# The second feed-forward's way up by seven half products, in two sweeps over pairs of token quarters

## The chip, the core and the metric

The kernel runs on one core of one Trainium2 chip. A core has TensorE for matrix products (PE in the profile, PEld for its weight loads), VectorE (DVE), ScalarE (ACT) and GpSimd (POOL) for elementwise work, and SyncE (SP), which issues the transfers here. Matrix products are summed in PSUM banks; all else lies in SBUF, or in DRAM. The metric is the device time of one execution in microseconds.

## The reference

One step of a transformer trunk layer on 1152 tokens (1024 latent, 128 context) of width 1024. What matters here is its end:

```python
def swiglu(h, w1, w3, w2):
    return (jax.nn.silu(h @ w1) * (h @ w3)) @ w2
...
    x = x + 0.5 * m[2] * swiglu(modulate(x, norm_g[0], m[0], m[1]), *ffn1)
    mix, ctx = token_mixer(modulate(x, norm_g[1], m[3], m[4]), cache, lb, *mixer_w)
    x = x + m[5] * mix
    x = x + 0.5 * m[8] * swiglu(modulate(x, norm_g[2], m[6], m[7]), *ffn2)
```

`w1` and `w3` are 1024 x 2816, `w2` is 2816 x 1024. `modulate` is an RMS norm with a gain and a shift that differ between latent and context tokens. The mixer ends in a merge: two gated up projections are added and go through `w_out`.

## The kernel before

Tokens lie along the free axis, features on the partitions: `x` is eight tiles of 128 x 1152. A product in fp32 accuracy is made of three matmuls in the fast rounded format (`float32r`): each operand is split into a rounded high part and the rest, and high x high, high x low and low x high are summed in one bank (`mm3`, L402; the three matmuls are L406, L407 and L408). A weight is loaded raw by `load_w` (L226), and `hl` (L215) makes its two parts: a cast on ScalarE (L222) and a subtraction on GpSimd (L223). The raw tile has two buffers, the parts (`wh`, `wl`) three each.

The whole runs in stages: first feed-forward, mixer (recurrence, then attention), merge, second feed-forward. The tile framework sorts each engine's queue when the program is built and sets the semaphores.

- `merge` (L1346) makes the up projections and gates tile by tile, three chunks of 384 tokens each, and adds `w_out`'s product to `x` in groups of two feature tiles (`down_group`), the last group chunk by chunk (`down_last`), after which `norm` (L341) makes the next stage's input `xh`, `xl`.
- `ffn` (L631) walks the 22 feature tiles of 128. For each, `up_plain` (L475) makes the gate's product in three chunks, its SiLU (L485), then the other product, their multiplication (L492), and splits the result into `hh`, `hl` (L493 on ScalarE, L494 on GpSimd). They stay in SBUF.
- After every two feature tiles `down_group` (L539) multiplies two older ones with their `w2` rows, 48 products, and adds them to `x` (`down`, L524, the addition on VectorE is L530). So up and down alternate, two feature tiles of each at a time.
- The last four feature tiles go through `down_final` (L571), which holds the final norm and stores the output.

Per feature tile the way up takes 2 x 3 x 24 matmuls of 384 columns, the way down 72.

Of the kernel before, what the change touches and what calls it, by code (L numbers as in the profile page):

```python
# [19 lines left out]
P = 128  # L20
# [16 lines left out]
LB_MIN = 1e-8  # L37

# [31 lines left out]
class Trunk:  # L70
# [3 lines left out]
    def run(self):  # L74
        self.part = {}
        nc, tc, a = self.nc, self.tc, self.a
        with ExitStack() as st:
# [16 lines left out]
            self.mixer()  # L94
            with ExitStack() as s1:
                self.ffn_pools(s1)
                self.ffn(1, 8, 3)
# [64 lines left out]
    def consts(self):  # L162
# [7 lines left out]
        self.mask = cp.tile([P, 5, P], U8, name="mask")  # L170
        mf = self.tt(F32, "maskf")[:, : 5 * P]
        nc.scalar.dma_start(mf, a["mask"])
        nc.vector.tensor_copy(self.mask.rearrange("p a b -> p (a b)"), mf)
        self.ones = cp.tile([P, P], F32, name="ones")
        nc.vector.memset(self.ones, 1.0 / D)
        self.onesb = cp.tile([P, P], F32, name="onesb")
        nc.vector.memset(self.onesb, 0.0)
        nc.vector.memset(self.onesb[0:64, 0:64], 1.0 / 64)
        nc.vector.memset(self.onesb[64:128, 64:128], 1.0 / 64)
        self.onesq = cp.tile([P, P], F32, name="onesq")  # L180
        nc.vector.memset(self.onesq, 1.0 / 384)
        self.onesk = cp.tile([P, P], F32, name="onesk")
        nc.vector.memset(self.onesk, 1.0 / 256)
# [31 lines left out]
    def hl(self, raw, shape, eng=None, pin=lambda i: i, pool=None):  # L215
        if pool:
            w = pool.tile([P, 2, *shape[1:]], F32R, tag="cb", bufs=1, name="wx")
            wh, wl = w[:, 0], w[:, 1]
        else:
            wh = self.wp.tile(shape, F32R, tag="wh", bufs=3, name="wh")  # L220
            wl = self.wp.tile(shape, F32R, tag="wl", bufs=3, name="wl")
# [94 lines left out]
    def rstd(self, r, ps, w=CW):  # L316
        nc = self.nc
        t = self.fp.tile([P, max(w, CW)], F32, tag="hf" if w <= CW else "sq", bufs=2 if w <= CW else 3, name="rt")[:, :w]
# [113 lines left out]
    def ffn_up(self, l, f):  # L432
# [4 lines left out]
        if self.plain:  # L437
            self.up_plain(l, f, hh, hl)
            return hh, hl
# [35 lines left out]
    def up_plain(self, l, f, hh, hl):  # L475
        nc = self.nc
        wa, wb = [partial(self.load_w, self.a["w13"][l, f, j], KT, P) for j in range(2)]

        def gate(c):
            if f or c != ORDER[0]:  # L480
                ps = self.dense(wa, c, "up", 3)
            else:
                ps = drain(self.dense_g(wa, c, "up", 3), self.tail)
            s = self.fp.tile([P, CW], F32, tag="sl", bufs=3, name="sl")
            nc.scalar.activation(s, ps, AF.Silu)  # L485
            return s

        def put(c, s):
            ps = self.dense(wb, c, "up", 3)
            cs = slice(c * CW, (c + 1) * CW)  # L490
            hf = self.fp.tile([P, CW], F32, tag="hf", bufs=2, name="hf")
            nc.vector.tensor_mul(hf, ps, s)  # L492
            nc.scalar.copy(hh[:, cs], hf)  # L493
            nc.gpsimd.tensor_sub(hl[:, cs], hf, hh[:, cs])  # L494
            self.tick()

        wa = wa()
        if f == 0:
            wb = wb()
            for c in ORDER:  # L500
                if c == ORDER[-1]:
                    for _ in self.tail:
                        pass
                s = gate(c)
                for _ in range(3):
                    next(self.tail, None)
                put(c, s)
                for _ in range(2):
                    next(self.tail, None)
        else:  # L510
            sl = [(c, gate(c)) for c in ORDER]
            wb = wb()
            for c, t in sl:
                put(c, t)

# [23 lines left out]
    def down_group(self, w2, fs, hs, gm):  # L539
        ws = [self.load_w(w2[f], 1, D) for f in fs]  # L540
# [966 lines left out]
```

## Time and profile before

| | us |
|---|---|
| median of three runs | 3118.07 |
| lowest and highest | 3117.59, 3119.81 |
| the profiled execution's own time | 3118.19 |
| its span in the trace | 3116.4 |
| merge begins in the trace (first matmul of `ups`) | 2038.5 |
| last matmul of the merge | 2251.0 |
| first matmul of the second feed-forward's way up | 2255.9 |
| last matmul of the way up | 3045.4 |

A group's row gives the line, the engine, the operation, output and inputs by the program's names, the shape and the count, then busy time in us and mean ns of one, then the idle time of the engine before them and what ended it. A row of the timeline gives start and duration in us. A matmul's duration in the trace includes its way through the array, some 0.17 us beyond its share of the array; the distance from one start to the next is what it costs in a stream. Rows with PEld are the weight loads that run beside it. The granted clock is 1.00 at full speed. Rows of the stages give a window, its length, then busy time and count of each engine, the clock, the share of the DMA engines and GB/s.

### The profile page before, as it was taken

How to read it: one execution, taken by the hardware profiler on the slowest of the kernel's cores; microseconds unless marked ns; L12 is line 12 of the kernel's file. 1: busy time of each engine (PE TensorE's matmuls, PEld its weight loads, DVE VectorE, ACT ScalarE, POOL GpSimd, SP SyncE). 2: the span in 40 equal slices, each digit the busy share in tenths (PEclk: the TensorE clock that was granted, in tenths of full speed). 3: DMA queues.
4: the chain of work that ended last, by engine and by line, in shares of the span. 5: the costliest groups of instructions: out<-in, count | busy, mean ns of one | idle time of the engine just before them, and what ended most of it. 6: DMA issues, size and time to landing. Idle time of an engine off the chain costs nothing.

```text
span 3116.4 us, 43157 instructions
## 1 busy us (share of the span) xinstructions
PE 2988.8 (96%) x16896; PEld 2840.4 (91%) x16896; DVE 1743.1 (56%) x3416; ACT 1093.8 (35%) x2029; POOL 1080.0 (35%) x864
## 2 busy tenths in 40 slices
PE   7999999999989999999998999999899999999998
PEld 5999999999988988898997777689899999999997
DVE  7867776675368777777546677744512222222224
ACT  4211111111165554545344777721531111111113
POOL 4322222222243333333235445554542222222224
PEclk9999999999999999999999999999999999999999
DMA  6322222221121111111110001242011111111111
GB/s 239 120 76 82 82 82 81 79 82 54 48 89 45 42 46 42 47 41 47 62 56 12 15 15 32 62 164 84 31 55 41 41 41 44 46 41 41 41 48 61
DMA packets 81211, 191.38 MB, mean 61 GB/s; under 512 B 11568, under 2 KB 36080, under 8 KB 80880
## 3 DMA queue, kind: packets, MB, share of 16 engines
q1 hardware_dynamic: 80864, 188.30, 17.6%
q8 instruction: 133, 2.18, 0.3%
q14 instruction: 70, 0.57, 0.1%
q10 hardware_dynamic: 144, 0.33, 0.0%
HBM read 165.17 MB, written 23.41 MB: 61 GB/s over the span
## 4 chain that ended last, share of the span: by engine, by line
PE 73%; DVE 15%; ACT 5%; issue 3%; POOL 2%; DMA 2%; SPq 0%; DVEq 0%; POOLq 0%; ACTq 0%
PE up L408 11%; PE up L407 11%; PE up L406 11%; PE dn L406 6%; PE dn L408 6%; PE dn L407 6%; PE mm L406 3%; PE mm L408 3%; PE mm L407 3%; DVE junk L273 2%; PE mps L1267 1%; DVE KE L909 1%; PE lv L898 1%; PE sps L1308 1%; PE sps L1310 1%
## 5 line engine op out<-in xcount | busy, mean ns | idle before, releaser
L223 POOL TENSOR_TENSOR wl<-raw,wh 128x1024 fp32r<-128x1024 f32 (+1 forms) x199 | 460.2, 2318 | 1095.7 <-ACT wh L222 1093.0
L406 PE MATMUL up<-xh,wh 128*128 128x384 f32 (+1 forms) x2088 | 708.7, 339 | 9.2 <-ACT wh L222 4.5
L407 PE MATMUL up<-xl,wh 128*128 128x384 f32 (+1 forms) x2088 | 707.6, 339 | 4.0 <-DVE xl L388 2.2
L408 PE MATMUL up<-xh,wl 128*128 128x384 f32 (+1 forms) x2088 | 708.4, 339 | 1.9 <-POOL wl L223 1.9
L222 ACT CAST wh<-raw 128x1024 fp32r<-128x1024 f32 (+1 forms) x201 | 200.0, 1005 | 761.8 <-PE dn L407 273.1
L530 DVE SCALAR_TENSOR_TENSOR x<-dn,modt,x 128x256 f32<-128x256 f32 (+1 forms) x704 | 346.9, 515 | 205.0 <-PE dn L408 204.4
L406 PEld LDWEIGHTS up<-xh,wh 128*128 128x128 f32 x2088 | 394.4, 189 | 13.2 <-ACT wh L222 6.6
L407 PEld LDWEIGHTS up<-xl,wh 128*128 128x128 f32 x2088 | 394.6, 189 | 8.3 <-DVE xl L388 5.6
L408 PEld LDWEIGHTS up<-xh,wl 128*128 128x128 f32 x2088 | 393.9, 189 | 2.6 <-POOL wl L223 2.4
L406 PE MATMUL mm<-xh,wh 128*128 128x384 f32 (+1 forms) x1008 | 360.5, 358 | 7.7 <-ACT wh L222 4.5
L406 PE MATMUL dn<-hh,wh 128*128 128x384 f32 (+2 forms) x1008 | 343.1, 340 | 20.6 <-DVE x L530 20.2
L408 PE MATMUL mm<-xh,wl 128*128 128x384 f32 (+1 forms) x1008 | 342.8, 340 | 1.7 <-POOL wl L223 1.7
L407 PE MATMUL mm<-xl,wh 128*128 128x384 f32 (+1 forms) x1008 | 342.9, 340 | 0.0
L408 PE MATMUL dn<-hh,wl 128*128 128x384 f32 (+2 forms) x1008 | 340.8, 338 | 1.5 <-POOL wl L223 1.5
L407 PE MATMUL dn<-hl,wh 128*128 128x384 f32 (+2 forms) x1008 | 340.6, 338 | 0.0
L492 DVE TENSOR_TENSOR hf<-up,sl 128x384 f32<-128x384 f32 x66 | 36.8, 557 | 502.5 <-PE up L408 502.5
L273 DVE SCALAR_TENSOR_TENSOR junk<-wada,cb 128x512 bf16<-128x512 f32 x224 | 262.6, 1173 | 12.1 <-DMA wada<-in_w_aT 6.2
L406 PEld LDWEIGHTS dn<-hh,wh 128*128 128x128 f32 x1008 | 190.9, 189 | 25.0 <-issue 23.0
L406 PEld LDWEIGHTS mm<-xh,wh 128*128 128x128 f32 (+1 forms) x1008 | 190.6, 189 | 16.8 <-ACT wh L222 4.8
L408 PEld LDWEIGHTS dn<-hh,wl 128*128 128x128 f32 x1008 | 190.6, 189 | 2.9 <-POOL wl L223 1.8
L408 PEld LDWEIGHTS mm<-xh,wl 128*128 128x128 f32 (+1 forms) x1008 | 189.8, 188 | 3.2 <-POOL wl L223 2.2
L407 PEld LDWEIGHTS dn<-hl,wh 128*128 128x128 f32 x1008 | 190.8, 189 | 1.7 <-issue 0.2
(355 smaller groups left out, 4965.3 us busy)
## 6 DMA issues: line engine op xcount, KB each, us to landing
raw<-in_w SPq DMA_DIRECT2D x132, 512.0 KB, 3.2
wada<-in_w_aT SPq DMA_DIRECT2D x112, 256.0 KB, 2.8
raw<-in_w_in SPq DMA_DIRECT2D x41, 512.0 KB, 3.3
sgates<-sg SPq DMA_DIRECT2D x48, 192.0 KB, 1.9
g<-sgates SPq DMA_DIRECT2D x48, 192.0 KB, 2.4
wada<-in_w_ada SPq DMA_DIRECT2D x16, 512.0 KB, 10.4
x<-in_xT SPq DMA_DIRECT2D x8, 576.0 KB, 10.9
xs<-x SPq DMA_DIRECT2D x24, 192.0 KB, 1.8
```

The costliest lines, as they stand in the source:

```text
L222: pin(self.nc.scalar.copy(wh, raw))
L223: pin((eng or self.nc.gpsimd).tensor_sub(wl, raw, wh))
L273: i = nc.vector.scalar_tensor_tensor(junk, w, 1.0, self.cb[:, s, cs], ALU.mult, ALU.mult, accum_out=o)
L406: nc.tensor.matmul(ps, wh, xh, start=start and i == 0, stop=False)
L407: nc.tensor.matmul(ps, wh, xl, start=False, stop=False)
L408: nc.tensor.matmul(ps, wl, xh, start=False, stop=stop and i == n - 1)
L492: nc.vector.tensor_mul(hf, ps, s)
L530: nc.vector.scalar_tensor_tensor(self.x[m][:, lo:hi], ps[:, lo - c * CW : hi - c * CW], self.modt[:, gm, m, s : s + 1], self.x[m][:, lo:hi ...
L898: nc.tensor.matmul(ps[:, j], kr[:, ts(j, P)], qp[:, ts(j, P)], start=True, stop=True)
L909: eng.tensor_tensor(v, v, bc(tt[r], m), ALU.mult)
L1267: nc.tensor.matmul(ps, q[0][0:96, qs], kt[0][0:96, ts(c, CW)], start=True, stop=True)
L1308: nc.tensor.matmul(ps, kt[0][R, ks], qh[R, qs], start=True, stop=False)
```

## The change

The product of the second feed-forward's way up is seen as a 2 x 2 block product: rows are gate (`w1`) and value (`w3`), the inner dimension is cut into two halves of 512, and the columns are two token quarters of 288. It is made from seven half products instead of eight, in Winograd's form of Strassen's method. The operands are sums of blocks: on the weights' side `a11`, `a12` (w1) and `a21`, `a22` (w3), with `s1 = a21 + a22`, `s2 = s1 - a11`, `a11 - a21` (written over `a21`) and `a12 - s2` (written over `a12`); on the tokens' side likewise. The products are numbered 1 to 7 and are made in the order 1, 6, 7, 5, 2, 4, 3. Some share a bank: 2 is added onto 1, 4 onto 7, 3 onto 5, after the earlier sum has been read out.

- **Two sweeps.** `ffn_fast` goes through all 22 feature tiles for quarters 0 and 2, then again for 1 and 3: 44 blocks of seven products, each 4 x 3 matmuls of 288 columns. The weights are loaded, summed and split again in the second sweep.
- **Weights** (`fast_ops`): a raw tile of 128 x 2 x 512 holds `a11` and `a21`, the other `a22` and `a12`; each has one buffer. A sum is made on GpSimd, every operand is cast on ScalarE, and its rest is taken on VectorE (product 1's on GpSimd). The next feature tile's first pair is loaded once product 7 is prepared, its second pair once product 3 is. Six operand pairs fit, and five are made ahead.
- **Tokens** (`norm_pair`): norm, sums and split of seven operands for each pair of quarters; the second pair's is interleaved with the first blocks of sweep one.
- **Evacuation** (`fast_block`): a copy, additions of the banks to SBUF tiles, two SiLUs and two multiplications per block; the results go to DRAM (`hs`), two stores per block.
- **The way down** no longer alternates with the way up: after both sweeps every feature tile's values are loaded (`load_h`), split (`split_h`), and go through `down_group`, whose form is the same. `x` is read back from DRAM too.
- **The merge** is made over quarters of 288 tokens, first all its up projections, then `w_out`; `x` is written to DRAM. Masks and constants of the mixer now live in a pool of its own.

The core of the diff:

```diff
+    def fast_ops(self, l, fs):
...
+        def load(f, i):
+            t = raws[i] = self.wp.tile([P, 2, 512], F32, tag="raw", bufs=2, name="raw")
+            for v, (j, h) in enumerate((((0, 0), (1, 0)), ((1, 1), (0, 1)))[i]):
+                src = self.a["w13"][l, f, j][:, 4 * h : 4 * h + 4].rearrange("p k m -> p (k m)")
+                nc.sync.dma_start(t[:, v], src)
...
+            (a11, a21), (a22, a12) = [(t[:, 0], t[:, 1]) for t in raws]
+            s1, s2 = [self.half("ws")[:, :512] for _ in range(2)]
+            src = {1: a11, 6: s2, 7: a21, 5: s1, 2: a12, 4: a22, 3: a12}
+            pre = {
+                6: ((s1, a21, a22, ALU.add), (s2, s1, a11, ALU.subtract)),
+                7: ((a21, a11, a21, ALU.subtract),),
+                3: ((a12, a12, s2, ALU.subtract),),
+            }
+            for i in PRODUCTS:
+                for o, x, y, op in pre.get(i, ()):
+                    nc.gpsimd.tensor_tensor(o, x, y, op)
+                t = self.wp.tile([P, 2, 512], F32R, tag=("wh", "wl")[n % 2], bufs=3, name="wo")
+                wh, wl = t[:, 0], t[:, 1]
+                n += 1
+                nc.scalar.copy(wh, src[i])
+                (nc.gpsimd if i == 1 else nc.vector).tensor_sub(wl, src[i], wh)
+                if j + 1 < len(fs) and i in (7, 3):
+                    load(fs[j + 1], int(i == 3))
+                yield [w.rearrange("p (k m) -> p k m", k=4) for w in (wh, wl)]
+
+    def fast_block(self, n, f, r):
...
+            for k in range(4):
+                for v, (w, x) in enumerate(((wh, xh), (wh, xl), (wl, xh))):
+                    first = home == i and k == 0 and v == 0
+                    last = k == 3 and v == 2
+                    nc.tensor.matmul(ps, w[:, k], x[:, k], start=first, stop=last, skip_group_check=home != i)
+            if i == 1:
+                nc.scalar.copy(t1, ps)
+            elif i == 6:
+                nc.vector.tensor_add(t1, ps, t1)
+            elif i == 7:
+                nc.vector.tensor_add(t2, ps, t1)
+            elif i == 5:
+                nc.vector.tensor_add(t2, ps, t2)
+            elif i == 2:
+                nc.scalar.activation(t3, ps, AF.Silu)
+            elif i == 4:
+                nc.vector.tensor_add(t4, ps, t1)
+                nc.vector.tensor_mul(t3, t3, t4)
+                put(t3, pr[0])
+            else:
+                nc.vector.tensor_add(t1, ps, t1)
+                nc.scalar.activation(t1, t1, AF.Silu)
+                nc.vector.tensor_mul(t1, t1, t2)
+                put(t1, pr[1])
...
+        for r in range(2):
+            for f in range(NF):
+                g = self.fast_block(r * NF + f, f, r)
...
+                for n in range(7):
+                    w = next(ops, None)
+                    if w:
+                        made.append(w)
+                    g.send(made.pop(0))
+                    if count % 10 == 0:
+                        next(self.tail, None)
...
+        for f in range(2, NF):
+            pend.append(split_h(*load_h(f)))
+            if f % 2 and f < NF - 1:
+                fs, hs = zip(*pend[:2])
+                self.down_group(w2, fs, hs, gm, ws)
+                pend, ws = pend[2:], None
```

How this stands on the engines, at three places. First VectorE, in the way up. Before, the last products of a feature tile are multiplied with the gate, and then the sums of a down group follow:

```order
L492 TENSOR_TENSOR hf_25562<-up_25537,sl_25475 128x384
L492 TENSOR_TENSOR hf_25591<-up_25566,sl_25502 128x384
L492 TENSOR_TENSOR hf_25620<-up_25595,sl_25529 128x384
L530 SCALAR_TENSOR_TENSOR x0_18861<-dn_25636,modt_104,x0_18861 128x256
L530 SCALAR_TENSOR_TENSOR x0_18861<-dn_25636,modt_104,x0_18861 128x128
L530 SCALAR_TENSOR_TENSOR x0_18861<-dn_25645,modt_104,x0_18861 128x384
```

Now, in sweep two. `wo` is an operand pair (its high part is an input of the subtraction that makes the low one), `b5`, `b6`, `b7` are banks, `et` a block's evacuation tile; `raw_25710` holds a22 and a12 of the next feature tile, `raw_25635` its a11 and a21, `ws_25728` is s2, `ws_25727` s1:

```order
L1466 TENSOR_TENSOR wo_25748<-ws_25728,wo_25748 128x512
L1466 TENSOR_TENSOR wo_25766<-raw_25635,wo_25766 128x512
L1466 TENSOR_TENSOR wo_25785<-ws_25727,wo_25785 128x512
L1506 TENSOR_TENSOR et_25688<-b7_25732,et_25688 128x288
L1507 TENSOR_TENSOR et_25688<-et_25688 128x288
L1466 TENSOR_TENSOR wo_25803<-raw_25710,wo_25803 128x512
L1510 TENSOR_TENSOR et_25688<-b5_25751,et_25688 128x288
L1466 TENSOR_TENSOR wo_25823<-raw_25710,wo_25823 128x512
L1512 TENSOR_TENSOR et_25688<-et_25688 128x288
L1466 TENSOR_TENSOR wo_25841<-raw_25710,wo_25841 128x512
```

The queue held evacuations alone; now the splits of the next block's operands 6, 7, 5, 2, 4 and 3 stand among the evacuations of this block's products 4 and 3 (L1506 to L1512).

Second GpSimd, at the same place. Before, the low parts of weights (L223) and of the results (L494):

```order
L223 TENSOR_TENSOR wl_25841<-raw_25838,wh_25840 128x1024
L494 TENSOR_TENSOR hl_25443<-hf_25620,hh_25442 128x384
L223 TENSOR_TENSOR wl_25928<-raw_25925,wh_25927 128x1024
L223 TENSOR_TENSOR wl_26023<-raw_26020,wh_26022 128x1024
L223 TENSOR_TENSOR wl_26110<-raw_26107,wh_26109 128x1024
```

Now, for the feature tile of the VectorE rows above:

```order
L1466 TENSOR_TENSOR wo_25729<-raw_25635,wo_25729 128x512
L1461 TENSOR_TENSOR ws_25727<-raw_25635,raw_25710 128x512
L1461 TENSOR_TENSOR ws_25728<-ws_25727,raw_25635 128x512
L1461 TENSOR_TENSOR raw_25635<-raw_25635 128x512
L1461 TENSOR_TENSOR raw_25710<-raw_25710,ws_25728 128x512
```

The weights' low parts have gone to VectorE but for product 1's, and four sums of raw blocks have come.

Third GpSimd in the way down. `wl` is the low part of a `w2` tile, `hl` that of a feature tile's values. Before, near the end of the stage, weights of the way up and down and results are mixed:

```order
L223 TENSOR_TENSOR wl_26417<-raw_26414,wh_26416 128x1024
L494 TENSOR_TENSOR hl_26019<-hf_26196,hh_26018 128x384
L223 TENSOR_TENSOR wl_26504<-raw_26501,wh_26503 128x1024
L223 TENSOR_TENSOR wl_26599<-raw_26596,wh_26598 128x1024
L223 TENSOR_TENSOR wl_26686<-raw_26683,wh_26685 128x1024
L494 TENSOR_TENSOR hl_26413<-hf_26532,hh_26412 128x384
```

Now:

```order
L225 TENSOR_TENSOR wl_27854<-raw_27851,wh_27853 128x1024
L225 TENSOR_TENSOR wl_28072<-raw_28069,wh_28071 128x1024
L1538 TENSOR_TENSOR hl_28508<-hr_28505,hh_28507 128x1152
L225 TENSOR_TENSOR wl_28078<-raw_28075,wh_28077 128x1024
L225 TENSOR_TENSOR wl_28296<-raw_28293,wh_28295 128x1024
```

Each group brings two weights of 1024 columns and one part of 1152 (the other group member's is made on VectorE), with nothing of the way up between them.

295 lines of the change are left out of this document (200 added, 95 removed).

## The prediction

> **What bounds the kernel now.** I read the page first, then the stages, then who waits for whom in the second feed-forward. The page:
>
> ```profile
> span 3116.4 us, 43157 instructions
> ...
> PE 2988.8 (96%) x16896; PEld 2840.4 (91%) x16896; DVE 1743.1 (56%) x3416; ACT 1093.8 (35%) x2029; POOL 1080.0 (35%) x864
> ...
> PE 73%; DVE 15%; ACT 5%; issue 3%; POOL 2%; DMA 2%; SPq 0%; DVEq 0%; POOLq 0%; ACTq 0%
> ```
>
> TensorE is busy 96% of the span and 73% of the chain that ends last. The stages from the mixer's end on: merge, entry of the second feed-forward, its body.
>
> ```profile
> 2038.00:2250.00 212.00, 206.53 (x1156) 204.14 (x1156) 91.07 (x174) 55.83 (x98) 98.28 (x79) 0.99 0.28 92
> 2250.00:2300.00 50.00, 40.93 (x202) 38.15 (x201) 20.55 (x24) 24.71 (x43) 29.67 (x22) 0.90 0.15 53
> 2300.00:3050.00 750.00, 750.00 (x4300) 750.00 (x4299) 177.60 (x351) 121.71 (x186) 208.45 (x124) 1.00 0.12 42
> ```
>
> In the third row TensorE is never idle: 4300 matmuls, nearly all 384 wide, in 750 us, so 0.1744 us each; VectorE has 178 us of work there, ScalarE 122, GpSimd 208. The others wait for TensorE:
>
> ```profile
> DVE hf L492 <- PE up L408: 502.5, 64, 16.3
> POOL wl L223 <- ACT wh L222: 441.4, 54, 21.1
> ```
>
> The body is bound by matmul columns alone, and weight preparation has hundreds of microseconds to spare. The change cuts columns and multiplies preparation.
>
> **The matmuls.** The narrowest wide matmuls now are 256 columns, in the last projection:
>
> ```profile
> 3093.28 0.28 PE L406 MATMUL dn<-hh,wh 128*128 128x256 f32 x1
> ...
> 3094.80 0.28 PE L407 MATMUL dn<-hl,wh 128*128 128x256 f32 x1
> ```
>
> Thirteen steps lie between these two: 1.52 / 13 = 0.117 us. 288 columns lie a quarter of the way from 256 to 384: 0.117 + 0.0575 / 4 = 0.1313 us. Removed: 22 x 2 x 3 x 24 = 3168 matmuls at 0.1744 = 552.5 us. Added: 2 x 22 x 84 = 3696 at 0.1313 = 485.3 us, 11.03 us for each of 44 blocks. If TensorE stays fed, that is -67.2 us. The merge keeps its columns (1536 at 0.1313 = 201.7 against 1152 at 0.1744 = 200.9), and the down projection its 1584 matmuls.
>
> **The preparation, block by block.** Before, a feature tile's two weights were cast and split once. Now every block splits seven half operands, four of them built by sums, and does it again in the second sweep. Its pieces are 128x512; the nearest rows are attention's cast and subtraction of just that shape (minimum/median/maximum in ns):
>
> ```profile
> L1317 POOL TENSOR_TENSOR ehl<-e,ehl x93: 1272/1291/1705, 1713.2 to 2032.9; 128x512 fp32r<-128x512 f32 x93
> L1317 DVE TENSOR_TENSOR ehl<-e,ehl x51: 673/692/1768, 1717.2 to 2037.6; 128x512 fp32r<-128x512 f32 x51
> L1315 ACT CAST ehl<-e x144: 607/620/629, 1712.4 to 2036.7; 128x512 fp32r<-128x512 f32 x144
> wada<-in_w_aT SPq DMA_DIRECT2D x112, 256.0 KB, 2.8
> L492 DVE TENSOR_TENSOR hf<-up,sl 128x384 f32<-128x384 f32 x66 | 36.8, 557 | 502.5 <-PE up L408 502.5
> L485 ACT ACTIVATE sl<-up 128x384 f32<-128x384 f32 x66 | 32.3, 489 | 138.7 <-PE up L408 138.7
> ```
>
> By throughput a block fits: ScalarE 7 x 0.62 and three 288-wide ops at about 0.42, 5.6 us; VectorE 6 x 0.69 and seven 288-wide ops at about 0.46 (a little over three quarters of 0.557), 7.4 us; GpSimd 5 x 1.29 = 6.5 us; all under 11.03. But the steps form a loop. The raw tile with a22 and a12 has one buffer: the next load waits until product 3, the last, is split, and the next block's product 6, its second, needs that load and two GpSimd sums before anything else. Between them VectorE takes its work in the order shown in the section on the change: splits 6, 7, 5, two evacuation ops of product 4, split 2, one of product 3, split 4, another of 3, split 3. On SyncE's queue the load of a22 stands behind the two stores of the block before, which are ready earlier. So once round:
> - load of a22, 256 KB: 2.8
> - two sums on GpSimd: 2 x 1.29 = 2.58
> - cast of operand 6: 0.62
> - six splits on VectorE: 6 x 0.69 = 4.14
> - four evacuation ops: 4 x 0.46 = 1.84
> - six handoffs between engines
>
> The handoffs I take from a chain that has no other wait in it:
>
> ```profile
> 3041.64 0.56 DVE L492 TENSOR_TENSOR hf<-up,sl 128x384 f32<-128x384 f32 x1 [3.64 <-PE up L408]
> ...
> 3042.23 0.51 ACT L493 CAST hh<-hf 128x384 fp32r<-128x384 f32 x1 [3.69 <-DVE hf L492]
> 3042.82 1.01 POOL L494 TENSOR_TENSOR hl<-hf,hh 128x384 fp32r<-128x384 f32 x1 [3.19 <-ACT hh L493]
> ```
>
> The multiplication ends at 3042.20 and the cast starts 0.03 later; the cast ends at 3042.74 and the subtraction starts 0.08 later. Six at the mean of 0.06: 0.35. So far 12.3 us, already more than TensorE's 11.03. Then VectorE and GpSimd get in each other's way:
>
> ```profile
> 2254.57 1.32 POOL L355 TENSOR_TENSOR xl<-xn,xh 128x384 fp32r<-128x384 f32 x1
> ...
> 2254.95 0.60 DVE L530 SCALAR_TENSOR_TENSOR x<-dn,modt,x 128x384 f32<-128x384 f32 x1
> ...
> 2255.89 2.64 POOL L223 TENSOR_TENSOR wl<-raw,wh 128x1024 fp32r<-128x1024 f32 x1
> 2256.28 2.67 DVE L339 TENSOR_TENSOR rs<-rs,sq 128x384 f32<-128x384 f32 x1
> 2231.63 0.55 DVE L339 TENSOR_TENSOR sb<-sb,sq 128x384 f32<-128x384 f32 x1
> ```
>
> The last row, from a quiet moment, is the 128x384 addition of the row above it: 0.55 alone, 2.67 when a GpSimd operation is under way, ending 0.42 behind that one. An operation of VectorE with both inputs in SBUF does not run beside one of GpSimd; the second row, whose input `dn` lies in PSUM, does. Twice a round this bites: split 6 stands behind GpSimd's a11-a21, which began when operand 6 was summed (1.29 less the cast and handoffs, less 0.13 of start: 0.42), and split 4 behind a12-s2, which can begin only after split 2 (1.29 + 0.06 less the 0.46 evacuation between, less 0.13: 0.76). ScalarE has the gate's SiLU between its casts of 7 and 5, so splits 7 and 5 wait for their casts, 0.19 and 0.36. Sum 1.73, and a round is 14.06 us. Hence 44 x 14.06 = 618.6 us for the sweeps: +66.1 us against 552.5, although TensorE's own work fell by 67.2. TensorE idles about 3 us in each block, in pieces under 1.5 us.
>
> Bounds of a round: without the two waits for GpSimd 12.9. Upwards, this row of a 512 KB load shows how late one can land:
>
> ```profile
> raw<-in_w SPq DMA_DIRECT2D x1, 512.0 KB, 4.5
> ```
>
> With 4.5 for 2.8, 15.8. I take 14.06, since the median landing comes from loads of the same size and row length.
>
> **Around the sweeps.** Entry: 202 matmuls in the 50 us of the second stage above would need 35; 15 us are lost to the norm. The new entry has the same steps on a pair of quarters before the first product; I take no difference, +-10. The second pair's operands are made during the first sweep: four rounds of two multiplications (576 wide, 0.73), three and four 288-wide subtractions on VectorE, 18.7 us, in the queue that the loop runs through. Between 0, if they fill its waits, and 19: +10. The stores of h and the second reading of the weights (to some 100 GB/s) run beside; the third stage used 12% of the DMA engines.
>
> **The down projection** loses its cover. Before, up matmuls of two feature tiles stood between two groups. Now the groups follow each other, and of the three weight buffers a group holds two: the next group's second weight can be cast only when this group has ended. It costs a cast and a subtraction of 1024 columns before TensorE can go on. Their times, from the body:
>
> ```profile
> 3045.60 1.05 ACT L222 CAST wh<-raw 128x1024 fp32r<-128x1024 f32 x1 [2.86 <-PE up L407]
> ...
> 3046.73 2.39 POOL L223 TENSOR_TENSOR wl<-raw,wh 128x1024 fp32r<-128x1024 f32 x1 [2.90 <-ACT wh L222]
> ```
>
> The merge ends with such a wait:
>
> ```profile
> 2198.64 0.69 PE L408 MATMUL dn<-mh,wl 128*128 128x384 f32 x1 [2.81 <-POOL wl L223]
> 2199.12 0.52 PE L407 MATMUL dn<-ml,wh 128*128 128x384 f32 x1
> 2199.44 0.52 PE L408 MATMUL dn<-mh,wl 128*128 128x384 f32 x1
> ...
> 2201.36 0.42 PE L408 MATMUL dn<-mh,wl 128*128 128x384 f32 x1
> 2201.62 0.34 PE L406 MATMUL dn<-mh,wh 128*128 128x384 f32 x1
> ```
>
> A turn costs 1.05 + 2.39 + handoffs 0.16 less the three matmuls already possible (0.52): 3.1 us. After the 2.81 us wait in the rows, nine matmuls came 0.32 apart instead of 0.174: another 1.3. Of nine turns I count eight at 4.4: +35 (0 if casts slip ahead, 40 at most). Reading h back for the first group: +5 (0 to 10).
>
> The Trainium skill (TensorE: Matmul & The Clock Gate, Part 1: The HAM clock gate) says that the array falls to half clock after at least one idle window of about 3.4 us. A wait of 3.1 would stay under it and a turn would cost 3.1, so 25 in place of 35; the rows above show half speed after 2.81, and I go by them.
>
> **Sum.** The profiled execution took 3118.2 us (span 3116.4, 1.8 around it), the median of the runs 3118.1, so it needs no correction. 3118.2 + 66.1 + 10 + 35 + 5 = 3234 us.
>
> **Rivals.**
> - *No waits for GpSimd* (0.15): the sums find gaps in VectorE's queue. 44 x 12.9 = 568, 3118 + 15 + 50 = 3183. For it: the evacuation ops read PSUM and are not held. Against: all six splits read SBUF twice.
> - *TensorE stays the bound, and it is faster* (0.07): the round shrinks under 11.03 and the sweeps take 485: 3118 - 67 + 50 = 3101. It breaks even at a round of 552.5 - 50 = 502.5, over 44, 11.4 us. The load would have to land in about 1.3 us with no wait for GpSimd, or the casts come two blocks ahead. Against: the 2.8 row, and one buffer.
> - *The clock falls in the sweeps* (0.13): waits close together also did it, in the entry of before:
>
> ```profile
> 2280.66 0.44 PE L406 MATMUL up<-xh,wh 128*128 128x384 f32 x1
> ...
> 2284.43 0.44 PE L406 MATMUL up<-xh,wh 128*128 128x384 f32 x1 [1.08 <-ACT xh L354]
> 2285.52 0.44 PE L407 MATMUL up<-xl,wh 128*128 128x384 f32 x1 [0.64 <-POOL xl L355]
> ...
> 2287.12 0.52 PE L406 MATMUL up<-xh,wh 128*128 128x384 f32 x1
> 2287.44 0.52 PE L407 MATMUL up<-xl,wh 128*128 128x384 f32 x1
> ...
> 2290.00 0.48 PE L406 MATMUL up<-xh,wh 128*128 128x384 f32 x1
> ```
>
> From the first row on only seven matmuls start in the 4.9 us ahead of the third; then, from 2287.12 to 2290.00, nine come 0.32 apart and cost 1.3 us more. TensorE's 3 us of slack a block would swallow one such stretch; if its evacuations come late for VectorE, 44 x 1.3 = 57 is added: 3290. The Trainium skill (same page, A second HAM failure mode: psum-queue depth-cycling) tells of kernels in which short idles between groups make the clock swing. Here a block idles 21%, and those rows 75% of 4.9 us (seven times 0.174 is 1.2), so I give it little.
>
> The forecast itself has 0.65. Range 3150 to 3310: below it lies the faster rival and the shortest rounds, above it 15.8 us rounds with everything else at its upper end. A measurement of this kernel tells about 0.2% from no change, 6 us. Faster 0.08 (the faster rival, and a hundredth for rounds near 11.4), within 0.2% 0.03 (such rounds again), slower 0.89.
>
> **What would show it.** Right: blocks about 14 us apart in the sweeps; TensorE near 79% there, waiting at product 6 for ScalarE's cast and VectorE's split; GpSimd's first sum waiting for the load; VectorE's splits 6 and 4 above 1 us; in the down projection a wait near 3 us for GpSimd every 25 us. Wrong: blocks 11 us apart with TensorE full; GpSimd's first sum never waiting for the load; no waits between the groups of the down projection.

## The result, and the profile after

| | before | after |
|---|---|---|
| median of four runs, us | 3117.83 | 3214.40 |
| lowest and highest, us | 3115.05, 3119.81 | 3212.61, 3217.72 |
| the profiled execution's span, us | 3116.4 | 3211.8 |
| way up: first to last matmul, us | (mixed with the way down) | 2261.0 to 2875.7 |

The changed kernel is slower: ratio 1.0312, 95% interval 1.0294 to 1.0329. The forecast was 3234. The page, with its row for the way up's matmuls and one row of DMA issues:

```profile
span 3211.8 us, 47117 instructions
...
PE 2983.6 (93%) x17806; PEld 2803.2 (87%) x17806; DVE 2106.1 (66%) x3939; ACT 1243.3 (39%) x2341; POOL 1255.0 (39%) x985
...
L1494 PE MATMUL b<-xo,wo 128*128 128x288 f32 x3696 | 534.2, 303 | 77.7 <-DVE et L1500 32.7
...
raw<-in_w SPq DMA_DIRECT2D x176, 256.0 KB, 3.1
```

VectorE has 363 us more to do than before and TensorE fell from 96% of the span to 93%. The two stages in question, sweeps and way down, in windows:

```profile
2261.00:2876.00 615.00, 535.09 (x3702) 506.52 (x3701) 394.23 (x616) 244.36 (x498) 305.64 (x236) 0.98 0.30 99
2876.00:3211.80 335.80, 297.07 (x1598) 283.62 (x1597) 196.54 (x359) 67.25 (x83) 109.50 (x57) 0.95 0.27 97
```

The sweeps take 615 us where 485 were priced for TensorE alone and 552.5 were removed; the granted clock is 0.98 there. It is not the same all along: 0.93 up to the twelfth block, where the second pair's operands are made, and 1.00 behind it.

```profile
2261.00:2432.00 171.00, 145.54 (x973) 139.37 (x973) 129.35 (x192) 81.38 (x174) 94.11 (x74) 0.93 0.27 91
2432.00:2876.00 444.00, 389.55 (x2731) 367.14 (x2729) 264.88 (x425) 162.98 (x326) 211.53 (x163) 1.00 0.31 102
```

ScalarE's copy of product 1 stands once in each block, so its starts measure blocks. The first row is the line's summary with first and last start; the second is the twelfth block's copy in the timeline:

```profile
L1496 ACT COPY et<-b x44: 374/381/384, 2264.0 to 2869.3; 128x288 f32<-128x288 f32 x44
```

```profile
2432.00 0.38 ACT L1496 COPY et<-b 128x288 f32<-128x288 f32 x1
```

From the first to the twelfth copy it is 168.0 us, eleven blocks of 15.3 us. From there to the last it is 437.3 us, 32 blocks of 13.67. One such round on VectorE, GpSimd and ScalarE (parts of the timeline, in the order 6, 7, 5, evacuations of 4, 2, evacuation of 3, 4, evacuation, 3):

```profile
2707.02 0.68 DVE L1466 TENSOR_TENSOR wo<-raw,wo 128x512 fp32r<-128x512 f32 x1
...
2713.93 1.10 DVE L1466 TENSOR_TENSOR wo<-ws,wo 128x512 fp32r<-128x512 f32 x1 [4.74 <-ACT wo L1465]
2715.16 0.69 DVE L1466 TENSOR_TENSOR wo<-raw,wo 128x512 fp32r<-128x512 f32 x1
2715.98 0.69 DVE L1466 TENSOR_TENSOR wo<-ws,wo 128x512 fp32r<-128x512 f32 x1
2716.59 0.45 DVE L1506 TENSOR_TENSOR et<-b,et 128x288 f32<-128x288 f32 x1
2717.07 0.46 DVE L1507 TENSOR_TENSOR et<-et 128x288 f32<-128x288 f32 x1
2717.45 0.69 DVE L1466 TENSOR_TENSOR wo<-raw,wo 128x512 fp32r<-128x512 f32 x1
2718.05 0.45 DVE L1510 TENSOR_TENSOR et<-b,et 128x288 f32<-128x288 f32 x1
2718.42 1.68 DVE L1466 TENSOR_TENSOR wo<-raw,wo 128x512 fp32r<-128x512 f32 x1
2720.03 0.45 DVE L1512 TENSOR_TENSOR et<-et 128x288 f32<-128x288 f32 x1
2720.40 0.68 DVE L1466 TENSOR_TENSOR wo<-raw,wo 128x512 fp32r<-128x512 f32 x1
```

```profile
2710.58 1.29 POOL L1461 TENSOR_TENSOR ws<-raw 128x512 f32<-128x512 f32 x1 [1.47 <-DMA raw<-in_w]
2711.95 1.29 POOL L1461 TENSOR_TENSOR ws<-ws,raw 128x512 f32<-128x512 f32 x1
2713.20 1.28 POOL L1461 TENSOR_TENSOR raw<-raw 128x512 f32<-128x512 f32 x1
2718.27 1.29 POOL L1461 TENSOR_TENSOR raw<-raw,ws 128x512 f32<-128x512 f32 x1 [3.79 <-issue]
```

```profile
2713.27 0.62 ACT L1465 CAST wo<-ws 128x512 fp32r<-128x512 f32 x1 [5.52 <-POOL ws L1461]
```

Follow it once round: split 3 ends at 2707.70 and the load is issued; GpSimd's first sum starts when it has landed, 2.88 later; the second sum ends at 2713.24, the cast of operand 6 follows at once, split 6 at 2713.93, and nine more operations of VectorE bring split 3 to its end at 2721.08. That is 13.38 us, and each step in it starts when another has ended. The round is one of the shorter ones: from the load's issue to the first sum it takes 2.86 us, where the median of 31 blocks (sums from 2451 to 2861) takes 3.19, and that about makes up the difference to the mean of 13.67. Splits 6 and 4 last 1.10 and 1.68 instead of 0.69: each starts while GpSimd is in a sum and ends after it.

The list of waits of the matmuls on this line (us, times) reads otherwise:

```profile
  DVE et L1500: 32.7, 40
  DVE wo L1466: 25.0, 40
  ACT wo L1465: 17.6, 34
```

The largest wait is for L1500, VectorE's evacuation of product 7, and not for an operand. (With the weight loads, which wait beside the matmuls, the same list has 74.6 us in 80 waits for L1500. That counts nearly every wait twice, and the expectations below use that figure.) That made a second theory: the products wait for their banks. Two more were that the sheer amount of work on the helpers is the limit, and, on record, that the clock falls. The last is out for the later blocks, by the 1.00 above.

In the way down, two of the turns between groups, and the clock of the ten microseconds behind each:

```profile
2970.79 0.44 PE L415 MATMUL dn<-hh,wl 128*128 128x384 f32 x1 [2.67 <-POOL wl L225]
...
2999.63 0.44 PE L415 MATMUL dn<-hh,wl 128*128 128x384 f32 x1 [2.67 <-POOL wl L225]
```

```profile
2970.00:2980.00 10.00, 9.05 (x50) 8.74 (x51) 7.31 (x13) 0.00 (x0) 3.08 (x2) 1.00 0.63 216
3000.00:3010.00 10.00, 10.00 (x50) 10.00 (x49) 7.50 (x13) 0.00 (x0) 1.91 (x1) 0.83 0.32 114
```

Equal waits, but only the second was followed by a lower clock.

### The profile page after: what moved, and what is told of

It is laid out like the page before. It is cut to its first block, busy times and chain, and to the rows that moved or that the text cites. A ratio compares the mean times of both kernels' runs of the same rounds, so it can differ in the third digit from the quotient of the medians.

```text
span 3211.8 us, 47117 instructions
## 1 busy us (share of the span) xinstructions
PE 2983.6 (93%) x17806; PEld 2803.2 (87%) x17806; DVE 2106.1 (66%) x3939; ACT 1243.3 (39%) x2341; POOL 1255.0 (39%) x985
## 5 line engine op out<-in xcount | busy, mean ns | idle before, releaser
L225 POOL TENSOR_TENSOR wl<-raw,wh 128x1024 fp32r<-128x1024 f32 (+2 forms) x164 | 378.1, 2311 | 696.6 <-ACT wh L224 693.8
L1494 PE MATMUL b<-xo,wo 128*128 128x288 f32 x3696 | 534.2, 303 | 77.7 <-DVE et L1500 32.7
L1494 PEld LDWEIGHTS b<-xo,wo 128*128 128x128 f32 x3696 | 505.9, 192 | 105.8 <-DVE et L1500 42.0
L224 ACT CAST wh<-raw 128x1024 fp32r<-128x1024 f32 (+2 forms) x166 | 163.6, 996 | 627.3 <-PE dn L414 418.9
L413 PE MATMUL up<-xh,wh 128*128 128x384 f32 (+1 forms) x1032 | 351.9, 341 | 2.8 <-DVE sl L457 1.4
L414 PE MATMUL up<-xl,wh 128*128 128x384 f32 (+1 forms) x1032 | 350.8, 340 | 2.1 <-DVE xl L395 1.7
L415 PE MATMUL up<-xh,wl 128*128 128x384 f32 (+1 forms) x1032 | 350.6, 340 | 0.0
L1466 DVE TENSOR_TENSOR wo<-ws,wo 128x512 fp32r<-128x512 f32 x88 | 78.9, 896 | 199.1 <-ACT wo L1465 194.2
L413 PEld LDWEIGHTS up<-xh,wh 128*128 128x128 f32 x1032 | 195.5, 189 | 5.3 <-ACT xh L394 1.7
L414 PEld LDWEIGHTS up<-xl,wh 128*128 128x128 f32 x1032 | 195.5, 189 | 5.1 <-DVE xl L395 4.9
```

Of the source, the lines that this page charges most:

```text
L224: pin(self.nc.scalar.copy(wh, raw))
L225: pin((eng or self.nc.gpsimd).tensor_sub(wl, raw, wh))
L413: nc.tensor.matmul(ps, wh, xh, start=start and i == 0, stop=False)
L414: nc.tensor.matmul(ps, wh, xl, start=False, stop=False)
L415: nc.tensor.matmul(ps, wl, xh, start=False, stop=stop and i == n - 1)
L1466: (nc.gpsimd if i == 1 else nc.vector).tensor_sub(wl, src[i], wh)
```

## The experiments

All are edits of the changed kernel. Ratios are to the kernel before, measured beside each group of runs (3119.2 us for the first four, 3119.8 for the next four, 3117.6 for the last three). The two columns on the right are from the traces, as above: the first eleven blocks together, and the mean of the 32 after them.

| run | us | ratio, 95% interval | first eleven | later block |
|---|---|---|---|---|
| changed kernel | 3214.4 | 1.0312, 1.0294 to 1.0329 | 168.0 | 13.67 |
| no reload of the weights | 3119.7 | 1.0003, 0.9994 to 1.0013 | 157.9 | 11.10 |
| first sum made twice | 3262.8 | 1.0457, 1.0442 to 1.0473 | 181.5 | 14.72 |
| four sums on VectorE | 3148.0 | 1.0089, 1.0072 to 1.0105 | 143.9 | 12.41 |
| a22 reloaded earlier | 3175.3 | 1.0179, 1.0164 to 1.0194 | 162.9 | 12.71 |
| buffers for the way down | 3188.1 | 1.0219, 1.0202 to 1.0236 | 169.9 | 13.77 |
| no operands of the second pair | 3208.8 | 1.0289, 1.0274 to 1.0305 | 154.9 | 13.80 |
| neither reload nor operands | 3090.4 | 0.9907, 0.9892 to 0.9922 | 127.3 | 11.11 |
| everything taken away | 3081.0 | 0.9880, 0.9865 to 0.9895 | 143.0 | 11.20 |
| sums ahead of 6 on VectorE | 3171.4 | 1.0174, 1.0157 to 1.0191 | 159.3 | 12.52 |
| sums for 7 and 3 on VectorE | 3201.9 | 1.0270, 1.0254 to 1.0285 | 163.9 | 13.38 |
| everything, operands in small steps | 3078.5 | 0.9873, 0.9858 to 0.9888 | 137.9 | 11.25 |

**Is it the loop? Taking a part of it away.**

```diff
-                if j + 1 < len(fs) and i in (7, 3):
-                    load(fs[j + 1], int(i == 3))
```

> Leaves out the reloading of the second feed-forward's up weights: the quarters of the first feature tile are loaded once and used for all 44 blocks, so the sums, splits, products and values follow from the wrong weights, and the number of instructions on every compute engine stays. Changed kernel 3214.4 us, 615 us in the sweeps, 13.65 us a block. Loop theory (a block lasts as long as its weights go round: landing, GpSimd's sums, cast, splits, casts after evacuations, the next reload): with the reload gone the round loses the 2.4 to 3.1 us landing and what is chained to it; TensorE's own work, 11.0 us a block, becomes the bound. About 44 x (13.65 - 11.1) = 112 us go: 3100 us, 3085 to 3125. Bank theory (the products wait for VectorE's reads of their PSUM banks, the largest of TensorE's waits in the trace, 74.6 us): those waits do not depend on the reload, so at least 75 us of waiting stays, and the time is 3180 to 3215.

94.7 us went, within the range, and a later block took 11.10 us. Every evacuation and every split is still made, and yet the matmuls' waits fall from 77.7 us to 21.5. This kernel's list (two lines less in the file, so L1498 is the L1500 of above):

```profile
  DVE et L1498: 10.5, 8
  ACT et L1494: 4.6, 3
  DVE et L1500: 4.1, 3
```

From the twelfth block on, the wait for this evacuation falls from 19.5 us to 0.8. The bank theory, which had it stay (the 75 us of the expectation are 32.7, counted once), is refuted. The wait for L1500 was the loop's delay seen from TensorE: the evacuation is late because VectorE's queue ahead of it is late, and the queue is late by the load.

**Lengthening it on an engine that is half idle.**

```diff
-                6: ((s1, a21, a22, ALU.add), (s2, s1, a11, ALU.subtract)),
+                6: ((s1, a21, a22, ALU.add), (s1, a21, a22, ALU.add), (s2, s1, a11, ALU.subtract)),
```

> The sum a21 + a22 is computed twice in a row on GpSimd for every block, with the same result; nothing is left out. Changed kernel 3214.4 us. Loop theory: the sum stands on the round between the landing and the cast of product 6, so each of 44 rounds becomes 1.0 to 1.3 us longer (1.29 us is the sum's duration in the trace), 44 to 57 us in all: 3257 to 3273 us. Throughput theory (what matters is how full the engines are; GpSimd is busy for 306 of the sweeps' 615 us, so 57 us more find room): no change, 3205 to 3225 us. Bank theory: no change either, as the instruction is on an engine that reads no bank.

48.4 us more, 1.05 for each later block. GpSimd is busy for 306 of 615 us, and one more instruction still costs 1.05 of its 1.29 us: the amount of work is not the limit, the place in the loop is.

**Where the sums are made.**

```diff
-                    nc.gpsimd.tensor_tensor(o, x, y, op)
+                    nc.vector.tensor_tensor(o, x, y, op)
```

> The four sums of the weights' quarters in each block are computed by VectorE in place of GpSimd; nothing is left out. Changed kernel 3214.4 us. Loop theory: a sum between two SBUF operands takes 1.29 us on GpSimd and about 0.67 us on VectorE, two sums stand on the round (-1.2 us), and VectorE's splits no longer run beside a GpSimd sum (the stretched ones of 1.10 and 1.68 us fall back towards 0.69 us, another -0.4 to -0.8 us at most); VectorE's queue gives some of it back, since a sum waits there behind evacuations. 13.65 - 1.0 to 1.25 us a block, 44 to 55 us less: 3160 to 3172 us. Rival, VectorE becomes late: 44 x 4 x 0.67 = 118 us are added to an engine that is busy for 507 of 615 us, which would be more than the stage has; its evacuations, which TensorE waits for, come later, and the time is 3215 to 3255 us.

66.4 us went, more than expected: the later blocks gave 1.26 us each, at the upper end of the forecast, 40 us for 32 of them, and the first eleven gave 24. The splits by their operand, first in the changed kernel, then here (busy us and mean ns behind the bar):

```profile
L1466 DVE TENSOR_TENSOR wo<-raw,wo 128x512 fp32r<-128x512 f32 x176 | 163.6, 930 | 5.8 <-ACT wo L1465 0.4
...
L1466 DVE TENSOR_TENSOR wo<-ws,wo 128x512 fp32r<-128x512 f32 x88 | 78.9, 896 | 199.1 <-ACT wo L1465 194.2
```

```profile
L1466 DVE TENSOR_TENSOR wo<-raw,wo 128x512 fp32r<-128x512 f32 x176 | 134.7, 785 | 6.3 <-ACT wo L1465 6.1
...
L1466 DVE TENSOR_TENSOR wo<-ws,wo 128x512 fp32r<-128x512 f32 x88 | 56.5, 681 | 0.7 <-ACT wo L1465 0.7
```

The same 264 splits lasted 51.3 us less together, 1.17 us a block, where the prediction had 0.42 + 0.76 = 1.18 of waiting for GpSimd. At 0.69 each they would last 182.2 us, so 60.3 us were stretch in the changed kernel and 9.0 are left here, where product 1's split is still GpSimd's. Part of what went is taken up again by the sums that now stand in VectorE's queue. The Trainium skill (SBUF — State Buffer, SBUF: two separate sides) calls the pair of ports that the two engines share an exclusive lock: an operation of VectorE with two SBUF inputs and one of GpSimd do not run side by side, and the later one waits to the end of the other. By that rule the stretch should go with the sums, and most of it went. The next two runs divide the edit.

```diff
-                    nc.gpsimd.tensor_tensor(o, x, y, op)
+                    (nc.vector if i == 6 else nc.gpsimd).tensor_tensor(o, x, y, op)
```

> Of the four sums of a block only the two ahead of product 6 (a21 + a22 and s1 - a11) are moved to VectorE; a11 - a21 and a12 - s2 stay on GpSimd. Nothing is left out. Changed kernel 3214.4 us, with all four on VectorE 3148.0. Theory: of that gain of 66 us the part for the faster sums on the round, 2 x (1.29 - 0.68) = 1.22 us a block, comes here, up to 54 us; GpSimd's two sums that are left still hold VectorE's splits and sums up, which can take back a part: 3160 to 3180 us. Rival (the whole gain came from splits that are no longer stretched): 3205 to 3216 us.

43.0 us went, as expected, and the collision with GpSimd shows in a new place. The second sum, now on VectorE beside GpSimd's a11 - a21, takes 1.6 us on average where the first takes 0.72:

```profile
L1461 DVE TENSOR_TENSOR ws<-ws,raw 128x512 f32<-128x512 f32 x44 | 71.1, 1617 | 0.0
...
L1461 DVE TENSOR_TENSOR ws<-raw 128x512 f32<-128x512 f32 x44 | 31.6, 718 | 86.0 <-DMA raw<-in_w 85.9
```

```diff
-                    nc.gpsimd.tensor_tensor(o, x, y, op)
+                    (nc.gpsimd if i == 6 else nc.vector).tensor_tensor(o, x, y, op)
```

> The counterpart: a11 - a21 and a12 - s2 go to VectorE, the two sums ahead of product 6 stay on GpSimd. Nothing is left out. Changed kernel 3214.4 us. Theory: the splits 6 and 4 no longer stand behind a GpSimd operation (0.42 + 0.76 = 1.18 us a block less), VectorE has two sums more in the round (2 x 0.68 = 1.36), of which some 0.2 fills its wait for a cast; the two cancel: 3205 to 3222 us. If the splits were not held up by GpSimd, only the added sums would count, 1.16 to 1.36 us a block, 51 to 60 us: 3262 to 3275 us.

12.5 us went, 3 us below the theory's range and 60 from the other case. So GpSimd did hold up the splits, whose means fall to 717 and 687 ns. The sum a11 - a21 was priced too high: it falls into VectorE's idle time ahead of split 6 (first fence, from the timeline), at the cost of stretching GpSimd's second sum, which runs beside it (second fence, from the groups):

```profile
2705.66 0.69 DVE L1461 TENSOR_TENSOR raw<-raw 128x512 f32<-128x512 f32 x1 [3.17 <-POOL ws L1461]
2708.18 0.69 DVE L1466 TENSOR_TENSOR wo<-ws,wo 128x512 fp32r<-128x512 f32 x1 [1.82 <-ACT wo L1465]
```

```profile
L1461 POOL TENSOR_TENSOR ws<-ws,raw 128x512 f32<-128x512 f32 x44 | 77.8, 1768 | 7.4 <-DVE sq L1386 4.1
L1466 DVE TENSOR_TENSOR wo<-ws,wo 128x512 fp32r<-128x512 f32 x88 | 60.5, 687 | 69.2 <-ACT wo L1465 69.2
```

**Starting the load earlier.** The load is given its two halves apart; the core of the edit:

```diff
-                if j + 1 < len(fs) and i in (7, 3):
-                    load(fs[j + 1], int(i == 3))
+                if j + 1 < len(fs) and i == 7:
+                    load(fs[j + 1], 0)
+                if j + 1 < len(fs) and i in (4, 3):
+                    load(fs[j + 1], 1, (int(i == 3),))
```

> The quarter a22 of the next feature tile is reloaded right after the split of product 4, its last reader, and no longer together with a12 after product 3; nothing is left out. Changed kernel 3214.4 us. Loop theory: the transfer of a22 starts one step (the cast and split of product 3, 0.62 + 0.69 us less their overlap with the step before) earlier, 1.0 to 1.3 us of 13.65 us, and the sum that waits for it with it: 44 to 57 us less, 3157 to 3170 us. Rival, the transfers share a queue and the second half lands when it landed before (the landing is counted with both halves of 128 KB together): 3205 to 3220 us. Bank theory: no change, 3205 to 3220 us.

39.1 us went, 5 less than the least expected. In the round above split 4 ends at 2720.10 and split 3 at 2721.08, 0.98 us apart, and a later block gave 0.96; the expectation had counted durations (0.62 + 0.69) that overlap with others. TensorE now waits once in a block, until ScalarE's SiLU has read the bank of product 2, and the rest of a block is one stream of 84 matmuls:

```profile
2702.56 11.41 PE L1499 MATMUL b<-xo,wo 128*128 128x288 f32 x84 [1.20 <-ACT et L1509]
```

**The turns of the way down.**

```diff
-        ws = ws or [self.load_w(w2[f], 1, D) for f in fs]
+        ws = ws or [self.load_w(w2[f], 1, D, pool=self.fp if self.late and n else None) for n, f in enumerate(fs)]
```

> The second weight of each group of the second way down gets buffers of its own, so its cast need not wait for the end of the group before; nothing is left out. Changed kernel 3214.4 us. In its trace the nine turns wait 1.15 to 2.77 us for GpSimd's subtraction, 19.8 us in all, and some of them are followed by matmuls at half clock. Theory (a turn is a weight that waits for a buffer): the waits go and the half clock with them, 27 to 32 us less: 3182 to 3188 us. Rival (GpSimd has work for the turn anyway, the values' splits of 1152 columns, and the wait only moves to them): 3204 to 3216 us.

26.3 us went between the medians, the upper edge of the range. In its trace the way down takes 303.9 us from its first matmul, after 336.0; its sweeps took 5 us longer this time and began 5 later. Some 1.7 of the 32.1 us lie in the first hundred matmuls, ahead of any turn. From the 101st to the 1461st the time was 273.9 (2901.74 to 3175.66) and is 243.5 (2910.66 to 3154.17): the nine turns, which all lie in this stretch, cost 30.4 us by these traces. The window that had the lower clock:

```profile
3000.00:3010.00 10.00, 10.00 (x59) 10.00 (x59) 6.61 (x15) 0.00 (x0) 3.58 (x2) 1.00 0.52 198
```

59 matmuls in place of 50, at full clock: with the waits the half clock is gone too.

**The second pair's operands.** The lines that make them go, and the second sweep takes the first pair's:

```diff
-                    if count % 10 == 0:
-                        next(self.tail, None)
...
-        X, pr = self.X[r], PAIRS[r]
+        X, pr = self.X[0], PAIRS[r]
```

> Leaves out the norm, the sums and the splits of the second pair of token quarters: the second sweep uses the first pair's operands. Changed kernel 3214.4 us. Its first eleven blocks, in which those operands are made, take 168.0 us, against 11 x 13.65 = 150.2 at the pace of the later blocks. Theory (the operands stand in the queues that the weights' round goes through): all blocks come at 13.65 us and 15 to 18 us go: 3196 to 3200 us. Rival (the first blocks are long because of the start of the sweep, its loads and the operands that were made ahead): 3208 to 3216 us.

Only 5.6 us went, which is the rival's range. The trace says why this decides little: the first eleven blocks did fall by 13.1 us, to 154.9, but the later ones were 0.13 us longer in this run, which takes 4 of it back, and that spread is in other runs too (13.77 with the way down's buffers, an edit that does not touch the sweeps). So the operands cost something between 6 and 13 us, and 3 to 5 of the eleven blocks' 17.6 us above the later pace have another cause, which was not looked into. The clock goes with the operands: 0.99 in the first eleven blocks here, 0.93 in the changed kernel, where the matmuls waited for up to 3.4 us in the blocks that make them. How much of the operands' cost is the clock no run separates.

The same in a kernel that has no reload:

> Leaves out both the reloading of the up weights and the second pair's operands, each as in the runs that left out one. Without the reload alone the time was 3119.7 us, late blocks at 11.20 us, the first eleven 157.9 us (34.7 more than at 11.20). Theory (without the reload TensorE is the bound, and the operands are no longer hidden): 30 to 38 us go, 3082 to 3090 us, all blocks near 11.1 us, the sweeps 488 to 494 us, so the 485 us that TensorE's columns were priced at are reached once it is fed. Rival (the first blocks are long for another reason): 3112 to 3120 us.

29.3 us went, just under what was expected: with TensorE as the bound nothing hides the operands. The sweeps last from 2263.7 to 2758.9 us, 495, of which the first block alone has 6.7 us above the pace of the others.

```profile
2400.00:2740.00 340.00, 340.00 (x2566) 340.00 (x2565) 291.42 (x398) 161.72 (x307) 212.98 (x152) 1.00 0.08 28
```

TensorE is never idle in this window: 2566 matmuls in 340 us are 0.1325 each, 11.13 a block. The prediction's 11.03 was right to 1%.

**Everything taken away, and nothing left out.** The edits of the earlier load, of VectorE's sums and of the way down, and from block 16 on this:

```diff
+        def ahead(f):
+            new = [[self.half("raw")[:, :512] for _ in range(2)] for _ in range(2)]
...
+            wide = more and j + 1 >= 16
+            if wide:
+                raws = ahead(fs[j + 1])
```

> All that the theory says costs time, taken away together, and nothing left out: a22 reloaded after product 4; from block 16 on the next feature tile's raw quarters go to four buffers of their own, loaded a whole block ahead; the four sums of a block on VectorE; buffers of their own for the way down's second weights. Changed kernel 3214.4 us, before 3119.2 us. Theory: blocks 16 to 43 at 11.2 to 11.5 us in place of 13.65 (28 x 2.3 = 64), the first 16 at 12.3 or so (about 1.3 each, 20), and 27 to 32 us of turns: 110 to 120 us less, 3094 to 3106 us, faster than both kernels. Rival (VectorE, with the sums then busy some 10 us of each 11, comes late with evacuations and splits, and blocks stay at 12 us or more): 3115 to 3135 us.

3081.0 us: 133.4 less than the changed kernel, and 38.8 less than before. The theory's account holds, and the surplus is in the first sixteen blocks: 199.2 us after 236.5, so 37 us where 20 were forecast. The last thirty of the 44 blocks in its trace:

```profile
2430.00:2771.00 341.00, 341.00 (x2561) 341.00 (x2560) 275.92 (x514) 167.55 (x303) 42.67 (x32) 1.00 0.40 126
```

TensorE is full, though VectorE has the sums as well and is busy for 276 of 341 us. So the seven half products do pay, by 1.2%, once the loop round the weights is shorter than TensorE's work. Which of the edits this takes is not shown: three rounds just ahead of block 16, still through the one set of raw buffers, took 11.37 us each (first sums at 2409.43 and 2443.54), and TensorE waited for nothing after 2411.19. No run has the other edits without the second set.

```diff
-            yield
+                if n % 1 == 0 or n == 6:
+                    yield
...
-                    if count % 10 == 0:
+                    if count % 3 == 0:
```

> The kernel with everything taken away (3081.0 us), and the second pair's operands made in 37 small pieces, one at every third product, in place of 9 lumps at every tenth; nothing is left out. Its first eleven blocks took 143.0 us against 11 x 11.2 = 123.2. Theory (a lump holds up the evacuations and splits queued behind it on VectorE and ScalarE, small pieces fit into the gaps): 6 to 16 us less, 3065 to 3075 us. Rival (VectorE has no room in a block in which it also makes sums and operands, however they are cut): 3078 to 3084 us.

2.5 us between the medians, with overlapping intervals: the rival. The first eleven blocks fell from 143.0 to 137.9, but the pieces now reach beyond them, and the 32 blocks after took 1.5 us more. Whether the operands come in lumps matters little.

## Why the prediction was right, and where its sizes were off

Against the 3118.2 us of the execution on which the sum was made:

| term | predicted | shown by the traces and runs |
|---|---|---|
| rounds, 44 blocks | +66.1 (14.06 us each) | +49.0 (13.67 each, 601.5 - 552.5) |
| second pair's operands | +10 | +13.2, all that the sweeps last beyond 44 such rounds: 17.6 in the first eleven blocks, less 4.4 since the last block has no round after it; 6 to 13 by the run without them |
| merge and all ahead of it | 0 | +9.8 (last matmul at 2260.84 for 2251.03) |
| entry | 0 | -15.0 |
| turns of the way down | +35 | +30.4 by the traces, 26.3 by the medians |
| reading h back and the start of the way down | +5 | +7.9, the rest of that stage |
| sum | +116 | +95, spans 3211.8 - 3116.4 |

Before, 860.5 us lay between the way up's first matmul and the end: 552.5, 1584 x 0.1744 = 276.3 for the way down, 10.3 of the 15 lost to the norm, and 21.4 at the very end. The last row but one is 336.0 less 276.3, 21.4 and 30.4.

**What held.** TensorE's saving exists (11.13 us a block when fed) and is not seen, since the preparation of weights is a loop through one buffer that is longer. Three runs lengthen, cut or shorten that loop and the time follows by about the amount of the step; two rivals, banks and amount of work, fail on the same runs. The collision of VectorE's splits with GpSimd's sums is real and near the predicted size: 0.41 + 0.99 us in the round above for 1.18, and 1.17 us a block went with the sums. At product 6 TensorE waits for the cast and the split, as forecast; the wait for the evacuation of product 7 was not forecast. The turns cost 30.4 us for 35.

**What was mis-sized: "six splits on VectorE: 6 x 0.69" and "four evacuation ops: 4 x 0.46".** A duration in the trace was taken for what an operation costs in a queue. In the round above, from split 6's start to split 3's end, 7.15 us passed; the prediction's terms for that stretch, 4.14 + 1.84 + 1.73, are 7.71. Seven operations in it follow straight on another, and six of these start 0.07 to 0.09 before the one ahead has ended (2717.45 after an end at 2717.53, 2718.42 after 2718.50), 0.45 together with the seventh. The waits for casts were 0.13 and 0.13 for 0.19 and 0.36, and split 4's was 0.99 for 0.76. The prediction had read handoffs between engines from starts and ends, but not those within an engine. The other way, the load's 2.8 us were a little short, by the 3.19 from issue to first sum.

**Entry and merge.** The 15 us that the norm cost before were assumed to come again, give or take 10. They did not, and the merge, for which nothing was added, came 9.8 later and took back two thirds of it. Before, 4.7 of the 15 lay ahead of the way up's first matmul and 10.3 behind it (194 matmuls, 33.8 us at 0.1744, in 44.1). Now the first product follows straight on the merge:

```profile
2255.90:2300.00 44.10, 39.53 (x194) 37.08 (x195) 14.79 (x16) 19.73 (x34) 25.41 (x18) 0.88 0.17 60
```

```profile
2260.84 0.30 PE L415 MATMUL ops<-mh,wl 128*128 128x288 f32 x1
2260.97 1.76 PE L1494 MATMUL b<-xo,wo 128*128 128x288 f32 x12
```

The merge begins 3 us later than before and takes 7 us longer; in it TensorE waits 10.0 us for VectorE's additions to `x` (L1377).

**The second pair's operands.** VectorE's work on them was priced at 18.7 us and took 35.6. The shortest rows are as priced (0.745 us at 576 columns for 0.73, 0.444 at 288 for 0.46), and the means are 0.94 and 1.00. GpSimd has every other split of theirs at the same time, so this may be the same collision; no run shows it by itself.

**The way down.** The turns' term is near, but not by its parts. Six of the turns waited 2.65 to 2.77 us and the others 1.15 to 1.36, where eight were priced at 3.1: 19.8 us for 24.8. The lower clock came behind four of them, where it was priced for all eight. Reading back cost a little more: the first matmuls waited 1.77 us for a split of 1152 columns on GpSimd and 2.95 for its cast:

```profile
2877.92 0.44 PE L414 MATMUL dn<-hl,wh 128*128 128x384 f32 x1 [1.77 <-POOL hl L1538]
2881.48 1.01 PE L413 MATMUL dn<-hh,wh 128*128 128x384 f32 x2 [2.95 <-ACT hh L1537]
```

**The rivals.** A kernel without waits for GpSimd would have been 3183: most of those waits went with the sums on VectorE, not in the changed kernel. Over the 32 later blocks the clock was 1.00, though TensorE idled 2.5 us of each; in the first eleven it was 0.93, and what that cost no run shows. The Trainium skill (TensorE: Matmul & The Clock Gate, A second HAM failure mode: psum-queue depth-cycling) tells of a clock that swings in kernels with short idles between groups; the 1.00 of the later blocks does not show it.

## What to carry to other kernels

Follow one buffer once round before counting how busy the engines are: with a single buffer, landing, sums, cast, split and the queue behind it add up, and an engine that is half idle can still set the pace. The releaser that a busy engine names most often may only hand on another's delay; lengthen or cut the suspected step by a known amount and see whether the time follows. A saving on the bound engine is worth its size only up to the next loop, so make that loop shorter first, here by an earlier reload, the sums on VectorE and a second set of raw buffers together.

## What the hardware showed beyond that

- The collision works both ways. GpSimd's sum of 1.31 us took 1.77 on average when a VectorE operation with both inputs in SBUF started just ahead of it, and VectorE's sum of 0.72 took 1.62 beside GpSimd.
- The lower clock after a wait is not certain: of six waits of 2.65 to 2.77 us in the way down four were followed by a window at 0.75 to 0.83, and two by 1.00. The Trainium skill (TensorE: Matmul & The Clock Gate, Part 1: The HAM clock gate) names at least one idle window of about 3.4 us; here shorter waits were enough, sometimes. What decides it no run shows.
- A transfer alone lands hardly sooner than one with another behind it on the queue. With a22's 256 KB (not 128, as the expectation has it) loaded by themselves GpSimd's first sum started 3.05 us after the issue (median of 30 later blocks), against 3.19 with a12's behind them (median of 31).
